# Earlier operands for the double blocks of a decoder's feed-forward stages, a one-step mean square, and a Silu placed ahead of the mixer's last linear

## The chip, the cores and the metric

The kernel runs on one core of a Trainium2 chip. Its engines work side by side, each through its own queue in order: TensorE (PE, with its weight loads listed as PEld), VectorE (DVE), ScalarE (ACT), GpSimd (POOL) and SyncE (SP, which issues the weight transfers). They meet through semaphores. The metric is the device time of one execution in microseconds; the kernel before takes 1538.5 us (median of 3 runs, 1538.31 to 1540.32).

## The reference

The kernel computes a decoder trunk of two layers on 256 tokens of width 1024, all in f32. With `D_FF = 2816`, each layer is

```python
x = x + 0.5 * swiglu(rmsnorm(x, norm_ffn1[i]), w_ffn1_up[i], w_ffn1_down[i])
h = rmsnorm(x, norm_mix[i])
x = x + token_mixers(h, ...)      # attention, gated recurrence, latent attention; gated, summed, @ w_out
x = x + 0.5 * swiglu(rmsnorm(x, norm_ffn2[i]), w_ffn2_up[i], w_ffn2_down[i])
gate = sigmoid(rmsnorm(x, norm_ple[i]) @ w_ple_gate[i])
x = x + gate * (p[i] @ w_ple_proj[i])
```

with a last `rmsnorm` behind both layers, and

```python
def rmsnorm(x, g): return x * rsqrt(mean(x * x) + EPS) * g
def swiglu(x, w_up, w_down):
    g, u = split(x @ w_up, 2)
    return (silu(g) * u) @ w_down
```

## The kernel before

**Split products.** PE multiplies numbers that are split in a high part (rounded) and a low part (the rest), three matmuls a product: `mm3` (L222 high by high, L223 high by low of the weights, L224 low by high). Each weight tile `raw` arrives by a transfer that SP issues; ACT casts it into `h` (L216) and DVE subtracts to get `l` (L217). The tiles of `h` and of `l` are pools of five, so a cast waits until PE has finished with the tile five before. Activations are split in the same way in `hl` (L229 cast on ACT, L230 subtraction on DVE).

**Feed-forward.** `ffn` goes through blocks of 256 hidden columns. A plain block multiplies the 256 tokens (two halves t = 0, 1) by its part of the up weights into `pu`; `hid` forms silu(g) * u (`sg` on ACT at L450, `hd` on DVE at L451); `hid_t` and `hl` transpose and split it into `fh`, `fl`; and `downs` adds the block before into `acc` with the down weights, two units `d` a block. In every stage but the first of layer 0 the blocks 2, 5 and 8 are double blocks (`wide_up`). These use fewer products: the inputs are seen as 2 by 2 parts a11, a12, a22 and four sums s1 to s4 of them, and the weights as parts `e` (the tiles of the pool we) and `o` (pool wo), each with a half lo and a half hi. Seven products, a11, s1, s2, s4, s3, a12, a22 in this order, each of 2 j by 2 q by 3 = 12 matmuls of 128x512, run against weight sums which `add` builds in place (L376, two DVE operations each, j = 0 and 1; 8 in a double block). In each product, for each j, ACT casts (L368), DVE subtracts (L369), PE multiplies; PE's lines L222 to L224 are the same as for a plain block. The names tell the product: `pu<-h,sh` are the products with sums.

**The activation sums.** `sums_x` (L321 to L337) forms the four sums once a stage from `rawx`, the scaled inputs before their split: L329 to L332 on DVE, each 128x512, then four casts `sh` (ACT) and four low parts `sl` (DVE, L230). It is called behind block 1, just ahead of the first double block. The second and third double block use the same sums.

**Norms.** `norm_sum` squares half a row on ACT (L417) with a sum; `norm_finish` adds the two half sums (L422 on DVE), `rsqrt` turns that into a mean plus EPS (L238 on DVE) and takes the power -1/2 on POOL (L239). There are 18 such roots of a whole row.

**Order.** The code is written in one order, but a scheduler with priorities places each instruction on its engine's queue, and it puts instructions that depend on little well ahead of where they stand in the code. So the order on an engine isn't the order of the code. ACT needs its function table switched between Silu, Exp, Ln and Sigmoid; each switch is an ACT_TABLE_LOAD in ACT's queue ahead of the activation that needs it.

Of the kernel before, what the change touches and what calls it, by code (L numbers as in the profile page):

```python
# [10 lines left out]
F32 = mybir.dt.float32  # L11
# [3 lines left out]
AF = mybir.ActivationFunctionType  # L15
OP = mybir.AluOpType
AX = mybir.AxisListType

DM, SEQ, DEPTH, DFF, PLE = 1024, 256, 2, 2816, 256
EPS = 1e-6  # L20
# [124 lines left out]
class Build:  # L145
# [206 lines left out]
    def wide_up(self, name, b):  # L352
        nc = self.nc
        e, o = self.wide_fetch(name, b)
# [6 lines left out]
        s1, s2, s3, s4 = self.sx_  # L361
# [12 lines left out]
        def add(d, dh, r, rh):  # L374
            for j in range(2):
                nc.vector.tensor_tensor(d[j][:, :, dh], d[j][:, :, dh], r[j][:, :, rh], op=OP.add)  # L376

        def keep(ps):
            c = self.tmt("pc")
            nc.scalar.copy(c, ps)  # L380
            return c
# [6 lines left out]
        p5 = keep(pb)  # L388
        add(e, lo, o, hi)
        prod(pa, s2, e, lo, False, False)  # L390
        u2 = keep(pa)
        prod(pb, s4, o, hi, False, True)
        nc.vector.tensor_tensor(u2, u2, pb, op=OP.add)
        add(e, hi, o, hi)
        prod(pa, s3, e, hi, False, False)
# [4 lines left out]
        mul(u2, u2, -1.0, p1, op0=OP.mult, op1=OP.mult)  # L400
        add(e, lo, o, lo)
        prod(pa, a22, e, lo, False, True)
# [10 lines left out]
    def norm_sum(self, t, half):  # L413
        nc = self.nc
        xs = self.x[:, t, half * 512:(half + 1) * 512]
        jk = self.tm.tile([128, 512], F32, name="jk", tag="tm")
        nc.scalar.activation(jk, xs, AF.Square, accum_out=self.ss[t][:, half:half + 1])  # L417

    def norm_finish(self, t):
        nc = self.nc  # L420
        s1 = self.small.tile([128, 1], F32, name="s1", tag="s1")
        nc.vector.tensor_tensor(s1, self.ss[t][:, 0:1], self.ss[t][:, 1:2], op=OP.add)  # L422
        self.rsqrt(self.rstd[t], s1, DM, 1)

# [3 lines left out]
    def ffn(self, name, gcol_next, mid=None, hook=None):  # L428
# [47 lines left out]
        for wide, b in plan(name, self.layer):  # L476
# [33 lines left out]
            hds = [hid(pu, t) for t in range(2)]  # L510
            if scaled and b == 0:
                sums = self.sums_x
            if b < FB - 1:
# [5 lines left out]
                self.hl(hh, ll, pt)  # L519
                if scaled and b == 1:  # L520
                    sums()
            else:
# [572 lines left out]
    def mixer(self, i, gcol_next):  # L1095
# [34 lines left out]

        self.scope.close()
        self.norm_begin_early(gcol_next)
        self.square_linear("w_out", consume)
# [167 lines left out]
```

## Time and profile before

| | value |
|---|---|
| median of the runs | 1538.5 us |
| profiled execution | 1538.71 us |
| its span, first to last instruction | 1536.9 us |
| mean granted clock of TensorE | 0.997 |
| PE / DVE / ACT busy | 1494.9 / 1113.8 / 925.9 us |
| HBM read over the span | 171 GB/s |
| chain that ended last | PE 82%, DVE 8%, ACT 7%, issue 2%, DMA 1% |

An engine's busy time is the sum of its instructions; for PE it holds the filling of the array too (0.39 us for a 128x512 matmul, while the next one starts some 0.23 us later), so a stall of PE is read from the distance of two starts. In the timelines, a bracket at the end of a row tells how long the engine was idle before it and which instruction released it. The granted clock is the share of full speed that TensorE had: 1.00 is 2.4 GHz, 0.50 is 1.2 GHz.

### The profile page before, as it was taken

The page shows a single profiled execution, that of the slowest core. Times are in us where ns is not written, and L with a number is a line of the kernel's source. Part 1 is how long each engine was busy: PE and PEld are TensorE (multiplying, and loading weights), DVE is VectorE, ACT ScalarE, POOL GpSimd, SP SyncE. Part 2 cuts the span into 40 slices and gives each one's busy share as a digit, 9 for nine tenths or more (in the row PEclk, how much of TensorE's full clock was granted, in tenths as well). Part 3 has the DMA queues.
Part 4 walks back from the last instruction along what each step waited for, and adds up shares of the span by engine and source line. Part 5 has one row for each costly group of instructions (what it writes and reads, how often), then busy time and mean ns, then how long its engine had stood idle before and what let it go on. Part 6 is the DMA issues. An engine that isn't in the chain of part 4 may idle for free.

```text
span 1536.9 us, 21608 instructions
## 1 busy us (share of the span) xinstructions
PE 1494.9 (97%) x8156; PEld 1235.3 (80%) x8156; DVE 1113.8 (72%) x1675; ACT 925.9 (60%) x1367; POOL 35.3 (2%) x48
## 2 busy tenths in 40 slices
PE   7999999999999998999999999999999999989997
PEld 6888888888888877888777888888888888778886
DVE  6555577677756679887788997676776566799876
ACT  6444486568565456656756665865775644656655
POOL 0000010000000000000000000100000000000000
PEclk9999999999999999999999999999999999999999
DMA  8666545344537553467535435553454385444462
GB/s 292 188 195 189 185 142 187 125 150 142 176 100 279 187 178 112 154 228 247 194 114 193 151 150 175 180 173 114 145 174 137 120 305 185 130 174 159 160 199 96
DMA packets 76473, 264.54 MB, mean 172 GB/s; under 512 B 8608, under 2 KB 9536, under 8 KB 76368
## 3 DMA queue, kind: packets, MB, share of 16 engines
q1 hardware_dynamic: 76144, 263.00, 51.1%
q8 instruction: 64, 1.05, 0.3%
q0 software_dynamic: 80, 0.11, 0.1%
q14 instruction: 41, 0.34, 0.1%
q10 hardware_dynamic: 144, 0.05, 0.0%
HBM read 262.08 MB, written 1.05 MB: 171 GB/s over the span
## 4 chain that ended last, share of the span: by engine, by line
PE 82%; DVE 8%; ACT 7%; issue 2%; DMA 1%; POOL 0%; SPq 0%; POOLq 0%; DVEq 0%; ACTq 0%
PE pu L223 18%; PE pu L222 18%; PE pu L224 18%; PE acc L223 5%; PE acc L224 5%; PE acc L222 5%; DVE l L369 2%; PE sq L224 2%; PE sq L223 2%; PE sq L222 2%; ACT h L216 2%; DVE l L217 1%; DVE wide L376 1%; PE pt L459 1%; ACT P L687 1%
## 5 line engine op out<-in xcount | busy, mean ns | idle before, releaser
L217 DVE TENSOR_TENSOR l<-raw,h 128x1024 fp32r<-128x1024 f32 (+3 forms) x440 | 512.6, 1179 | 230.9 <-ACT h L216 224.0
L216 ACT CAST h<-raw 128x1024 fp32r<-128x1024 f32 (+4 forms) x439 | 438.6, 1011 | 241.7 <-PE pu L224 132.5
L222 PE MATMUL pu<-h,xth 128*128 128x512 f32 (+3 forms) x1160 | 450.5, 389 | 12.7 <-DVE h L216 5.9
L223 PE MATMUL pu<-l,xth 128*128 128x512 f32 (+3 forms) x1160 | 442.2, 381 | 6.5 <-DVE l L369 4.4
L224 PE MATMUL pu<-h,xtl 128*128 128x512 f32 (+3 forms) x1160 | 439.4, 380 | 1.0 <-DVE xtl L230 1.0
L222 PEld LDWEIGHTS pu<-h,xth 128*128 128x128 f32 x1160 | 218.9, 189 | 53.2 <-ACT xth L232 5.9
L223 PEld LDWEIGHTS pu<-l,xth 128*128 128x128 f32 x1160 | 219.0, 189 | 43.8 <-DVE l L369 5.3
L224 PEld LDWEIGHTS pu<-h,xtl 128*128 128x128 f32 x1160 | 218.6, 188 | 39.1 <-DVE xtl L230 2.2
L368 ACT CAST h<-wide 128x1024 fp32r<-128x1024 f32 x126 | 126.6, 1051 | 65.8 <-PE acc L224 40.8
L369 DVE TENSOR_TENSOR l<-wide,h 128x1024 fp32r<-128x1024 f32 x126 | 147.9, 1220 | 9.3 <-ACT h L368 9.0
L223 PE MATMUL acc<-l,fh 128*128 128x512 f32 x352 | 138.1, 392 | 0.0
L224 PE MATMUL acc<-h,fl 128*128 128x512 f32 x352 | 137.7, 391 | 0.0
L222 PE MATMUL acc<-h,fh 128*128 128x512 f32 x352 | 134.1, 392 | 0.0
L376 DVE TENSOR_TENSOR wide<-wide 128x1024 f32<-128x1024 f32 x72 | 85.6, 1220 | 0.5
L223 PEld LDWEIGHTS acc<-l,fh 128*128 128x128 f32 x352 | 66.1, 188 | 15.1 <-DVE l L217 1.5
L224 PEld LDWEIGHTS acc<-h,fl 128*128 128x128 f32 x352 | 66.1, 188 | 13.3
L222 PEld LDWEIGHTS acc<-h,fh 128*128 128x128 f32 x352 | 66.1, 188 | 13.3
L223 PE MATMUL pu<-l,sh 128*128 128x512 f32 x144 | 58.2, 404 | 6.6 <-DVE l L369 5.6
L222 PE MATMUL pu<-h,sh 128*128 128x512 f32 x144 | 56.2, 397 | 1.6 <-ACT h L368 1.6
L224 PE MATMUL pu<-h,sl 128*128 128x512 f32 x144 | 56.8, 395 | 0.0
L223 PE MATMUL pu<-l,fh 128*128 128x512 f32 x128 | 50.8, 397 | 0.0
L222 PE MATMUL pu<-h,fh 128*128 128x512 f32 x128 | 50.4, 394 | 0.2 <-ACT pp L578 0.2
(269 smaller groups left out, 1821.8 us busy)
## 6 DMA issues: line engine op xcount, KB each, us to landing
raw<-in_weights_dram SPq DMA_DIRECT2D x374, 512.0 KB, 4.5
wide<-in_weights_dram SPq DMA_DIRECT2D x72, 512.0 KB, 5.5
raw<-in_weights_dram SPq DMA_DIRECT2D x48, 384.0 KB, 3.2
raw<-in_weights_dram SPq DMA_DIRECT2D x8, 320.0 KB, 3.1
raw<-in_weights_dram SPq DMA_DIRECT2D x8, 256.0 KB, 2.7
xin<-in_xt_dram SPq DMA_DIRECT2D x4, 256.0 KB, 7.7
x<-in_x_dram SPq DMA_DIRECT2D x2, 512.0 KB, 9.7
out_dram<-o SPq DMA_DIRECT2D x4, 256.0 KB, 2.2
```

The lines of the kernel that those rows point to most:

```text
L216: (copy or nc.scalar.copy)(h[:, :m], raw[:, :m])
L217: nc.vector.tensor_tensor(l[:, :m], raw[:, :m], h[:, :m].bitcast(F32), op=OP.subtract)
L222: mm(out, ah, bh, start=start, stop=False, skip_group_check=skip)
L223: mm(out, ah, bl, start=False, stop=False, skip_group_check=skip)
L224: mm(out, al, bh, start=False, stop=stop, skip_group_check=skip)
L368: nc.scalar.copy(h, src)
L369: nc.vector.tensor_tensor(l, src, h.bitcast(F32), op=OP.subtract)
L376: nc.vector.tensor_tensor(d[j][:, :, dh], d[j][:, :, dh], r[j][:, :, rh], op=OP.add)
L459: nc.tensor.transpose(pt[:, f, t * 128:(t + 1) * 128], hd[:, f * 128:(f + 1) * 128], self.ident)
L687: nc.scalar.activation(P[n, o], P[n, o], AF.Exp, bias=q[:, 3:4], scale=A_SCALE, accum_out=q[:, 4 + n:5 + n])
```

## The change

Three edits. First, `sums_x` is called behind block 0 instead of block 1, and in `wide_up` the third and the fourth weight sum are each written one product or more earlier, as soon as the tile that they overwrite has been read. Second, the scale 1/1024 of the mean goes into the squaring on ACT, and one DVE operation forms the mean and adds EPS, in place of two. Third, ahead of the norm and of the linear `w_out` at the end of the mixer stands a Silu of a one-column constant, whose result nothing uses.

```diff
@@ -387,18 +387,18 @@
         prod(pb, s1, e, lo, True, False)
         p5 = keep(pb)
         add(e, lo, o, hi)
+        add(e, hi, o, hi)
         prod(pa, s2, e, lo, False, False)
         u2 = keep(pa)
+        add(e, lo, o, lo)
         prod(pb, s4, o, hi, False, True)
         nc.vector.tensor_tensor(u2, u2, pb, op=OP.add)
-        add(e, hi, o, hi)
         prod(pa, s3, e, hi, False, False)
         u3 = keep(pa)
         prod(pc, a12, o, lo, True, True)
         nc.vector.tensor_tensor(p1, p1, pc, op=OP.add)
         nc.scalar.activation(p1, p1, AF.Silu)
         mul(u2, u2, -1.0, p1, op0=OP.mult, op1=OP.mult)
-        add(e, lo, o, lo)
         prod(pa, a22, e, lo, False, True)
         nc.vector.tensor_tensor(p5, p5, u3, op=OP.add)
         nc.scalar.activation(u3, pa, AF.Silu)
@@ -414,13 +414,13 @@
         nc = self.nc
         xs = self.x[:, t, half * 512:(half + 1) * 512]
         jk = self.tm.tile([128, 512], F32, name="jk", tag="tm")
-        nc.scalar.activation(jk, xs, AF.Square, accum_out=self.ss[t][:, half:half + 1])
+        nc.scalar.activation(jk, xs, AF.Square, scale=DM ** -0.5, accum_out=self.ss[t][:, half:half + 1])
 
     def norm_finish(self, t):
         nc = self.nc
-        s1 = self.small.tile([128, 1], F32, name="s1", tag="s1")
-        nc.vector.tensor_tensor(s1, self.ss[t][:, 0:1], self.ss[t][:, 1:2], op=OP.add)
-        self.rsqrt(self.rstd[t], s1, DM, 1)
+        ms = self.small.tile([128, 1], F32, name="ms", tag="ms")
+        nc.vector.scalar_tensor_tensor(ms, self.ss[t][:, 0:1], EPS, self.ss[t][:, 1:2], op0=OP.add, op1=OP.add)
+        nc.gpsimd.tensor_tensor(self.rstd[t], ms, self.mhalf[:, :1], op=OP.pow)
 
     def xmm(self, out, t, k, rh, rl, start, stop):
         self.mm3(out, self.xth[t][:, k, :], self.xtl[t][:, k, :], rh, rl, start, stop)
@@ -508,8 +508,6 @@
                     self.pending()
                 up(q, t)
             hds = [hid(pu, t) for t in range(2)]
-            if scaled and b == 0:
-                sums = self.sums_x
             if b < FB - 1:
                 if prev is not None:
                     downs()
@@ -517,8 +515,8 @@
                 for t in range(2):
                     hid_t(pt, hds[t], t)
                 self.hl(hh, ll, pt)
-                if scaled and b == 1:
-                    sums()
+                if scaled and b == 0:
+                    self.sums_x()
             else:
                 for pb, hT in prev[:-1]:
                     d0 = down_units(pb)
@@ -1129,6 +1127,8 @@
             self.norm_after(t, half)
 
         self.scope.close()
+        warm = self.small.tile([128, 1], F32, name="warm", tag="s1")
+        nc.scalar.activation(warm, self.mhalf[:, :1], AF.Silu)
         self.norm_begin_early(gcol_next)
         self.square_linear("w_out", consume)
```

How this moves instructions is read from the order on the engines. The first place is DVE in the second feed-forward stage of layer 0, from the `hd` of block 0's second half (`xs` are the sums, `sl` their low parts, `fl` the low part of the hidden values, `wide` the tiles e and o). Before:

```order
L451 TENSOR_TENSOR hd_5334<-pu_5237,sg_5333 128x256
L217 TENSOR_TENSOR l_5431<-raw_5428,h_5430 128x1024
L230 TENSOR_TENSOR fl_5263<-pt_5337,fh_5262 128x512
L217 TENSOR_TENSOR l_5437<-raw_5434,h_5436 128x1024
L369 TENSOR_TENSOR l_5515<-wide_5499,h_5514 128x1024
L376 TENSOR_TENSOR wide_5499<-wide_5499 128x2x512
L376 TENSOR_TENSOR wide_5499<-wide_5499,wide_5505 128x2x512
L451 TENSOR_TENSOR hd_5421<-pu_5344,sg_5420 128x256
L369 TENSOR_TENSOR l_5525<-wide_5502,h_5524 128x1024
L451 TENSOR_TENSOR hd_5425<-pu_5345,sg_5424 128x256
L329 TENSOR_TENSOR xs_5475<-xr1_5288 128x512
L376 TENSOR_TENSOR wide_5502<-wide_5502 128x2x512
```

After:

```order
L451 TENSOR_TENSOR hd_5324<-pu_5227,sg_5323 128x256
L329 TENSOR_TENSOR xs_5334<-xr1_5278 128x512
L217 TENSOR_TENSOR l_5445<-raw_5442,h_5444 128x1024
L230 TENSOR_TENSOR fl_5253<-pt_5327,fh_5252 128x512
L330 SCALAR_TENSOR_TENSOR xs_5335<-xs_5334,xr0_5174 128x512
L331 TENSOR_TENSOR xs_5336<-xr0_5174,xr1_5278 128x512
L332 SCALAR_TENSOR_TENSOR xs_5337<-xr0_5174,xs_5335 128x512
L230 TENSOR_TENSOR sl0_5343<-xs_5334,sh0_5342 128x512
L230 TENSOR_TENSOR sl1_5347<-xs_5335,sh1_5346 128x512
L230 TENSOR_TENSOR sl2_5351<-xs_5336,sh2_5350 128x512
L230 TENSOR_TENSOR sl3_5355<-xs_5337,sh3_5354 128x512
L217 TENSOR_TENSOR l_5451<-raw_5448,h_5450 128x1024
```

The sums and their low parts stood behind the two `hd` of block 1 and between the weight sums; now they stand directly behind the `hd` of block 0, ahead of the second down unit's `l` and of the double block's first.

The second place is DVE further on, in the same double block. The tiles of e are wide_5499 and wide_5502 before, wide_5489 and wide_5492 after; those of o are wide_5505 and wide_5508, then wide_5495 and wide_5498. Before:

```order
L376 TENSOR_TENSOR wide_5499<-wide_5499,wide_5505 128x2x512
L376 TENSOR_TENSOR wide_5502<-wide_5502,wide_5508 128x2x512 x2
L369 TENSOR_TENSOR l_5563<-wide_5499,h_5562 128x1024
L369 TENSOR_TENSOR l_5573<-wide_5502,h_5572 128x1024
L369 TENSOR_TENSOR l_5585<-wide_5505,h_5584 128x1024
L369 TENSOR_TENSOR l_5595<-wide_5508,h_5594 128x1024
L369 TENSOR_TENSOR l_5608<-wide_5499,h_5607 128x1024
L369 TENSOR_TENSOR l_5618<-wide_5502,h_5617 128x1024
L393 TENSOR_TENSOR pc_5582<-pc_5582,pu_5511 128x512
L369 TENSOR_TENSOR l_5630<-wide_5505,h_5629 128x1024
L369 TENSOR_TENSOR l_5640<-wide_5508,h_5639 128x1024
L376 TENSOR_TENSOR wide_5499<-wide_5499,wide_5505 128x2x512
```

After:

```order
L369 TENSOR_TENSOR l_5529<-wide_5489,h_5528 128x1024
L376 TENSOR_TENSOR wide_5492<-wide_5492,wide_5498 128x2x512
L230 TENSOR_TENSOR fl_5385<-pt_5482,fh_5384 128x512
L369 TENSOR_TENSOR l_5539<-wide_5492,h_5538 128x1024
L376 TENSOR_TENSOR wide_5489<-wide_5489,wide_5495 128x2x512
L376 TENSOR_TENSOR wide_5492<-wide_5492,wide_5498 128x2x512
L369 TENSOR_TENSOR l_5555<-wide_5489,h_5554 128x1024
L369 TENSOR_TENSOR l_5565<-wide_5492,h_5564 128x1024
L376 TENSOR_TENSOR wide_5489<-wide_5489,wide_5495 128x2x512
L376 TENSOR_TENSOR wide_5492<-wide_5492,wide_5498 128x2x512
L369 TENSOR_TENSOR l_5579<-wide_5495,h_5578 128x1024
L369 TENSOR_TENSOR l_5589<-wide_5498,h_5588 128x1024
```

In both orders six weight sums stand ahead of the `l` of s2 (l_5563 and l_5573 before, l_5555 and l_5565 after). The last two, which stood behind the `l` of a12 (l_5630, l_5640), now stand ahead of the `l` of s4 (l_5579, l_5589).

The third place is ACT in the attention part of the mixer of layer 0 (`ckh` and `kpeT` belong to the latent attention's keys, `PT` and `P` to the window attention's softmax). Before:

```order
L232 ACTIVATE ckh<-pt,gains 128x128
L705 COPY PT<-pt 128x384
L232 ACTIVATE ckh<-pt,gains 128x128
L954 COPY kpeT<-pt 64x128 x2
L232 ACTIVATE ckh<-pt,gains 128x128
L747 ACTIVATE bf<-pu,rstd 128x512
L705 COPY PT<-pt 128x384
L216 CAST h<-raw 128x768 x3
L229 CAST fh<-po 128x256
L687 ACTIVATE P,sta<-P,sta 128x384 x2
```

After:

```order
L1131 ACT_TABLE_LOAD
L1131 ACTIVATE warm<-mhalf 128x1
L232 ACTIVATE ckh<-pt,gains 128x128
L703 COPY PT<-pt 128x384
L232 ACTIVATE ckh<-pt,gains 128x128
L952 COPY kpeT<-pt 64x128 x2
L745 ACTIVATE bf<-pu,rstd 128x512
L232 ACTIVATE ckh<-pt,gains 128x128
L703 COPY PT<-pt 128x384
L216 CAST h<-raw 128x768 x3
L229 CAST fh<-po 128x256
L685 ACT_TABLE_LOAD
```

The one-column Silu `warm` does not stand ahead of `w_out`: it depends on a constant alone and stands in the mixer's middle, with a table load of its own, and the softmax behind it has a load that it did not have. In layer 1 it is the same, and the load at L450 stands in the order as before.

## Rows read from the trace of the kernel before

**Rows 1.** Page, busy time, share of the span and instructions of each engine
```profile
PE 1494.9 (97%) x8156; PEld 1235.3 (80%) x8156; DVE 1113.8 (72%) x1675; ACT 925.9 (60%) x1367; POOL 35.3 (2%) x48
```

**Rows 2.** Table of waits of PE: us in total, times, longest us
```profile
PE pu L223 <- DVE l L369: 10.0, 7, 1.8
```

**Rows 3.** Timeline of PE: start, us, instruction, [idle before <-releaser]
```profile
559.67 0.50 PE L222 MATMUL pu<-h,xth 128*128 128x512 f32 x1 [1.44 <-ACT xth L229]
...
577.58 0.39 PE L223 MATMUL acc<-l,fh 128*128 128x512 f32 x1
...
585.32 0.39 PE L222 MATMUL pu<-h,sh 128*128 128x512 f32 x1
585.81 0.50 PE L223 MATMUL pu<-l,sh 128*128 128x512 f32 x1
...
589.16 0.50 PE L222 MATMUL pu<-h,sh 128*128 128x512 f32 x1 [0.56 <-ACT h L368]
...
591.48 0.50 PE L223 MATMUL pu<-l,sh 128*128 128x512 f32 x1 [1.82 <-DVE l L369]
...
602.40 0.49 PE L222 MATMUL pu<-h,xth 128*128 128x512 f32 x1
...
604.36 0.50 PE L223 MATMUL pu<-l,xth 128*128 128x512 f32 x1 [1.46 <-DVE l L369]
```

**Rows 4.** Stretches: us; PE, PEld, DVE, ACT, POOL busy; PEclk; DMA; GB/s
```profile
582.50:607.00 24.50, 20.56 (x87) 15.59 (x85) 24.36 (x26) 16.80 (x22) 0.00 (x0) 1.00 0.19 62
811.00:816.00 5.00, 4.74 (x14) 3.74 (x15) 5.00 (x6) 3.52 (x5) 0.00 (x0) 0.66 0.00 0
```

**Rows 5.** Timeline of DVE, a first double block, layer 0
```profile
566.83 0.41 DVE L451 TENSOR_TENSOR hd<-pu,sg 128x256 f32<-128x256 f32 x1
...
570.29 1.23 DVE L217 TENSOR_TENSOR l<-raw,h 128x1024 fp32r<-128x1024 f32 x1 [1.20 <-ACT h L216]
572.52 1.23 DVE L369 TENSOR_TENSOR l<-wide,h 128x1024 fp32r<-128x1024 f32 x1 [1.01 <-ACT h L368]
...
577.98 0.68 DVE L329 TENSOR_TENSOR xs<-xr 128x512 f32<-128x512 f32 x1
...
581.53 2.49 DVE L230 TENSOR_TENSOR sl<-xs,sh 128x512 fp32r<-128x512 f32 x4
...
590.21 6.90 DVE L369 TENSOR_TENSOR l<-wide,h 128x1024 fp32r<-128x1024 f32 x6
```

**Rows 6.** Groups by line: busy us, mean ns, idle before <-releasers; the roots
```profile
L239 POOL TENSOR_TENSOR rstd<-ms,mhalf 128x1 f32<-128x1 f32 x18 | 9.9, 551 | 1073.4 <-ACT xth L232 566.9 <-DVE ms L238 486.7 <-ACT h L216 19.8
```

**Rows 7.** Timeline of DVE, the end of the program
```profile
1531.41 0.16 DVE L422 TENSOR_TENSOR s<-ss 128x1 f32<-128x1 f32 x1
1531.60 0.15 DVE L238 TENSOR_SCALAR ms<-s 128x1 f32<-128x1 f32 x1
```

**Rows 8.** Timeline of ACT, feed-forward stages
```profile
557.43 1.28 ACT L450 ACT_TABLE_LOAD   x1 [0.40 <-PE pu L224]
558.73 0.38 ACT L450 ACTIVATE sg<-pu 128x256 f32<-128x256 f32 x1
...
767.09 0.72 ACT L295 ACTIVATE xs<-x,rstd 128x512 f32<-128x512 f32 x1 [0.68 <-POOL rstd L239]
```

**Rows 9.** Timeline of ACT in the mixers of both layers
```profile
328.17 0.37 ACT L232 ACTIVATE ckh<-pt,gains 128x128 fp32r<-128x128 f32 x1 [0.67 <-DVE ckl L233]
...
329.89 0.48 ACT L705 COPY PT<-pt 128x384 f32<-128x384 f32 x1 [1.36 <-PE pt L700]
...
340.44 0.62 ACT L687 ACTIVATE P<-P,sta 128x384 f32<-128x384 f32 x1 [2.02 <-DVE sta L685]
...
1090.81 0.48 ACT L705 COPY PT<-pt 128x384 f32<-128x384 f32 x1 [1.52 <-PE pt L700]
```

**Rows 10.** Timeline of ACT, casts of the first double block
```profile
571.44 1.05 ACT L368 CAST h<-wide 128x1024 fp32r<-128x1024 f32 x1 [1.18 <-PE pu L224]
574.16 1.06 ACT L368 CAST h<-wide 128x1024 fp32r<-128x1024 f32 x1 [1.67 <-PE pu L224]
```


## The prediction

> **What bounds the kernel now.** I read the page's busy line first [rows 1]: TensorE (PE) is busy 1494.9 of 1536.9 us, VectorE (DVE) 1113.8. So an edit is worth only what it takes from PE's gaps; work taken off DVE or ScalarE (ACT) is worth nothing by itself. Next the table of waits for PE [rows 2]: its largest entry is PE at L223 waiting for `l` of L369, 10.0 us in 7 waits. That is one place of the program, met three times: the first double block of each of the three feed-forward stages that have double blocks. Then PE's own rows there [rows 3]. A 128x512 matmul starts every 0.23 us (from 591.48 to 602.40 there are 47 steps, 10.92 / 47 = 0.232), so each longer distance is a stall: 585.32 to 585.81 (0.49, stall 0.26), 585.81 to 589.16 (3.35 for 11 steps, which are 2.55: stall 0.8), 589.16 to 591.48 (2.09) and 602.40 to 604.36 (1.73), together 4.9 us. Two of these rows carry a wait for L369, 1.82 + 1.46 = 3.28; three such places make 9.8 of the 10.0 us of [rows 2], so the other two stages have the same stalls, and 3 x 4.9 = 14.7 us hang on the three places.
>
> Who is late there? The table of stretches [rows 4] says that DVE is busy 24.36 of the 24.50 us from 582.5 to 607, ACT only 16.80. DVE is simply behind. Its rows just before [rows 5] show where the time for it lies: between 566.83 and 577.98 it idles 1.20 us (before 570.29) and 1.01 us (before 572.52), for casts of ACT; then, where PE is about to need weight sums, it does four activation sums and their four low parts.
>
> **The double blocks, worked out.** The change puts these eight small operations behind the `hd` of 566.83, into the two idle stretches, and puts the last two weight sums (L376) ahead of the `l` of product s4; the six others already stand ahead of that of s2. DVE does the same operations as before; what it gains is the idle it no longer has, 1.20 + 1.01 = 2.2 us. The second and third double blocks of a stage get no sums, and their instructions on DVE stand practically as before; I count them at 0.
>
> What PE gets from it depends on the order, so I walk DVE's new order from 566.83 without idle up to the `l` of the third product's first half (row `l_5579` in the order after). That is 17 large operations (2 of L217, 7 of L369, 8 of L376), 10 small ones (4 sums, 4 `sl`, 2 `fl`), and 3 `hd`. From [rows 5]: a large one 6.90 / 6 = 1.15, a small one 2.49 / 4 = 0.62, an `hd` 0.41. So 17 x 1.155 + 10 x 0.62 + 3 x 0.42 = 19.6 + 6.2 + 1.3 = 27.1, and DVE reaches the end of that `l` at 593.9.
>
> On PE: product s1 starts at 585.32 as now, without its 0.26, and takes 12 x 0.23 = 2.75, so s2 could start at 588.1. The `l` of its second half comes 13 large, 10 small and 3 `hd` after 566.83, 22.5 us, at 589.3: about 1.0 of stall is left in s2. The next product's second matmul would then start near 592.0 and waits for the `l` at 593.9: a stall of 1.9. Behind it 36 matmuls lead to the second matmul of the last product, 36 x 0.232 = 8.4, at 602.3, with the later `l` just in time, against 604.36 now. So the block gains about 2.1 and keeps 1.0 + 1.9 of its 4.9. In words: the moved sums take the wait of 1.73 away from the last product and open one of 1.9 in the one after s2, since the last two weight sums now stand ahead of its `l`; what is left as a gain is DVE's recovered idle. Three times: **-6.3**. The bounds: 0 if DVE finds another wait where the idle was, 4.9 a block (-14.7) if every stall goes. I take the walk since it is made of measured durations and ends at the idle's own size.
>
> What hides the moved operations is the distance to what they now stand ahead of: the `l` of 570.29 moves to about 574.0 to 575.2, and PE, by [rows 3], meets it first at 577.58: 2.4 us of cover. If that cover were gone, each microsecond there would come straight back.
>
> **One step in the mean square.** 18 roots [rows 6] lose one small DVE operation each; from 1531.41 to 1531.60 [rows 7] the step takes 0.19. At the end nothing runs beside it: 0.19 in full. In the first feed-forward stage of layer 1 ACT idles 0.68 for the root at 767.09 [rows 8], and the other half of the tokens has the like: 2 x 0.19. In the other places casts or the table load of [rows 8] end later than the root; I give them 0.1 together. Sum **-0.7**, bounds 0 and 18 x 0.19 = 3.4.
>
> **The early Silu table.** The text of the change puts a one-column Silu ahead of the last linear of the mixer, so that the load at 557.43 (1.28 us, [rows 8]), for which PE waits 1.44 at 559.67 [rows 3], would be done before. The order says otherwise: the scheduler puts this activation, which depends on nothing but a constant, into the attention part of the mixer, near 328 in layer 0 and 1090 in layer 1. Exp, Ln and Sigmoid come behind it, and the load at L450 still stands before `sg`. So nothing is gained there, and each layer gets two more loads: the one for this Silu and one back to Exp at the softmax (L685 after). Both wait for nothing. The first falls where ACT idles 0.67 and 1.36 [rows 9]: 2.03 against 1.28 + 0.2, the 0.2 for the one-column activation being an estimate from DVE's one-column step of 0.19. The second falls into the 2.02 before 340.44. In layer 1 the idle before 1090.81 is 1.52. I take 0.25 a layer for the copy that comes later, **+0.5**; the bounds are 0 and all four on the path, 4 x (1.28 + 0.2) = 5.9.
>
> One rule speaks against that and gets a sum of its own. The row shows a load of 1.28 at 557.43 and the activation that needs it at 558.73, 0.02 behind its end [rows 8]. The Trainium skill, page "ScalarE: Activation LUTs", section "What ACT_TABLE_LOAD costs", states some 1283 ns for the load and another 1380 ns for a drain, 2.66 us for every switch. The load agrees with the row, the drain does not show in it. By the page four more switches would be up to 10.6 us where the rows allow 5.9.
>
> **The sum.** -6.3 - 0.7 + 0.5 = -6.5, from the profiled execution of 1538.71 (span 1536.9 and 1.8 around it): 1532.2; the median 1538.5 lies 0.2 lower, so **1532**. One thing I leave out of the sum: at 811 to 816 the granted clock was 0.66 on average [rows 4], that is at 1.2 instead of 2.4 GHz for about two thirds of these 5 us, right behind PE's stall; that lost some 1.7 us. The same stall at 591 and 1352 left the clock at full. If the new, shorter stalls leave it alone, 1530.5; if it falls in one more block, 1533.7.
>
> **Rivals.**
> 1. *All of it works*: 14.7 of stalls and three loads of 1.28 (3.8) go, and 0.7, and the 1.7 of the clock: 1518 (1538.7 - 14.7 - 3.8 - 0.7 - 1.7 = 1517.8). For it: every stall in [rows 3] waits for DVE or ACT. Against it: DVE has 24.36 of 24.50 us of work in the stretch, and only 2.2 of idle ahead; the order keeps the load.
> 2. *The added loads land on PE's path* in the mixer. For it: at 340.44 ACT and DVE work in turns on the softmax [rows 9], so a delay of ACT is handed on. Against it: the idle is there, and both loads come without a wait. Price 5.9 in place of 0.5: 1532 + 5.4 = 1537.4, no change.
> 3. *Each added switch stops ACT for as long again as its load*, 2 x 1.28, and the idle is too short for it: 4 x 2.56 = 10.2 in place of 0.5, 1542. For it no row speaks; against it is the 0.02 between load and use. The page of the Trainium skill named above is where this rule stands.
> 4. *Slower: the fourth sum sticks in ACT's queue.* ACT works in order, and in the new order a cast of the double block stands between the third `sh` and the fourth. Before, such casts wait for PE to give a buffer back: 1.18 until 571.44, the next 1.67 until 574.16 [rows 10]. The walk has `sl3` due near 573.2, right behind the cast of 571.44. If the cast ahead of the fourth `sh` is released one product later, everything behind `sl3` on DVE is 2.7 late, and the block loses 2.7 - 2.1 = 0.6: 1540; two releases later, 3.3 a block: 1538.7 - 0.2 + 10 = 1548. It decides as soon as the last `sh` comes over 2.1 us later than 573.2. Against it: the order of the casts among themselves is unchanged.
>
> **Chances.** Forecast 0.75, with its own range 1529.5 to 1535; rival 1 0.04; rival 2 0.13; rival 3 0.02; rival 4 0.05; 0.01 for none of these. A measurement of this kernel tells about 0.2% (3.1 us) from no change; so faster means under 1535.4. That is the forecast and rival 1: 0.79; no change is rival 2 and half of the rest: 0.15; slower is rivals 3 and 4 in part: 0.06. The range takes the forecast and, upward, rival 2 in most of its size: 1529 to 1537.
>
> **What the new profile would show.** Right: the `hd` at 566.83 followed by `xs` at once, no idle of over 0.5 us in DVE between 567 and 594; in s2 a stall near 1.0, in s4 one near 1.9, in the last product none, and the first double block's last product some 2 us earlier in each of the three stages; two more table loads per layer, at L1131 and L685, in ACT's idle, and the load at L450 still there with PE's wait at 559.67; the last step 0.19 shorter. Wrong: DVE waiting for `sh` of ACT near 573; PE waiting in the last product still; PE's waits in the mixer (330 to 360, 1090 to 1120) grown by over 1 us; or a clock under full in more than one of the three blocks.

## The result and the profile after

| | before | changed |
|---|---|---|
| median, runs beside each other | 1538.4 us (4 runs, 1537.73 to 1540.32) | 1527.55 us (4 runs, 1526.94 to 1527.86) |
| profiled execution, span | 1538.71, 1536.9 us | 1527.65, 1525.8 us |
| mean granted clock | 0.997 | 0.998 |

The ratio is 0.992, interval 0.9908 to 0.9932. Forecast was 1532.0 with a range of 1529 to 1537: faster, as said, but 11 us and not 6.5, and outside the range.

The busy line of the page after (engines in the columns of [rows 1]):

```profile
PE 1491.4 (98%) x8156; PEld 1234.8 (81%) x8156; DVE 1109.5 (73%) x1657; ACT 933.3 (61%) x1373; POOL 37.9 (2%) x48
```

Busy times hardly moved, so the 11 us are idle time of PE. The table of PE's waits says which (waiting and releasing line, us in total, times, longest):

```profile
PE pu L222 <- ACT xth L229: 4.5, 4, 1.4
PE pu L223 <- DVE l L369: 2.6, 8, 0.4
PE pu L222 <- ACT pc L380: 2.2, 3, 0.7
```

The 10.0 us of [rows 2] for `l` of L369 are 2.6 now, and a new wait of 2.2 us for ACT's copy `pc` stands beside it. The wait for `xth` behind the table load (4.6 before, of which [rows 3] shows one of 1.44) has stayed.

PE in the first double block of the second feed-forward stage of layer 0, which answers to [rows 3] (start, duration, instruction, idle before and releaser):

```profile
585.49 0.39 PE L222 MATMUL pu<-h,sh 128*128 128x512 f32 x1
...
588.21 0.39 PE L222 MATMUL pu<-h,sh 128*128 128x512 f32 x1
589.01 0.50 PE L223 MATMUL pu<-l,sh 128*128 128x512 f32 x1 [0.41 <-DVE l L369]
...
592.74 0.51 PE L222 MATMUL pu<-h,sh 128*128 128x512 f32 x1 [0.72 <-ACT pc L380]
...
593.59 0.50 PE L223 MATMUL pu<-l,sh 128*128 128x512 f32 x1 [0.35 <-DVE l L369]
...
601.68 0.39 PE L223 MATMUL pu<-l,xth 128*128 128x512 f32 x1
...
612.00 0.39 PE L222 MATMUL pu<-h,xth 128*128 128x512 f32 x1
```

The stall of 589.01 is 0.80 - 0.23 = 0.57, those of 592.74 and 593.59 are 0.88 and 0.62 (0.85 - 0.23), and the last product waits for nothing: its second matmul starts at 601.68 instead of 604.36. In this way, distance of two starts less 0.23, the stalls of the three first double blocks are 4.8 us each before and 2.1 us each after. The wait for `pc` costs nothing by itself: the matmul behind it waits for `l` until 593.59 in any case.

The length of a block says the same. From the first matmul of product s1 it is 110 matmuls to the one at 612.00 above, and in the trace before to this one:

```profile
614.78 0.40 PE L222 MATMUL pu<-h,xth 128*128 128x512 f32 x1
```

That is 614.78 - 585.32 = 29.46 us before and 612.00 - 585.49 = 26.51 us after. In the other two stages the same distance is 31.03 and 29.39 before (the first of them with the clock at half for a part) and 26.56 and 26.51 after. So each block is 2.9 to 3.0 us shorter, a little more than its stalls, since the steps just behind a stall are longer too (0.34 instead of 0.23).

DVE in the same place, which answers to [rows 5]:

```profile
567.02 0.42 DVE L451 TENSOR_TENSOR hd<-pu,sg 128x256 f32<-128x256 f32 x1
567.36 0.68 DVE L329 TENSOR_TENSOR xs<-xr 128x512 f32<-128x512 f32 x1
...
571.50 0.68 DVE L230 TENSOR_TENSOR sl<-xs,sh 128x512 fp32r<-128x512 f32 x1
573.91 1.22 DVE L217 TENSOR_TENSOR l<-raw,h 128x1024 fp32r<-128x1024 f32 x1
...
587.73 1.22 DVE L369 TENSOR_TENSOR l<-wide,h 128x1024 fp32r<-128x1024 f32 x1
...
592.32 1.22 DVE L369 TENSOR_TENSOR l<-wide,h 128x1024 fp32r<-128x1024 f32 x1
```

The sums stand right behind `hd`, all four `sl` follow without a gap, and from 567.02 to 596.86 no bracket appears: the two idle stretches of [rows 5] are filled. The `l` of product s4 starts at 592.32 and is done at about 593.5.

The stretches of [rows 4] (us, busy time of PE, PEld, DVE, ACT, POOL, then granted clock, DMA share, GB/s):

```profile
582.50:607.00 24.50, 23.02 (x101) 18.10 (x99) 24.29 (x26) 18.13 (x22) 0.00 (x0) 1.00 0.29 101
805.00:812.00 7.00, 5.94 (x24) 4.32 (x24) 7.00 (x7) 6.42 (x8) 0.00 (x0) 1.00 0.00 0
```

PE is busy 23.02 of 24.50 us where it was 20.56. The second row is the stretch behind the stalls of the second block, which come some 6 us earlier now (804.79 to 809.38): its clock is 1.00, where the stretch behind the stall, 811 to 816, had 0.66.

ACT in the mixer and at the first silu, which answers to [rows 9] and [rows 8]:

```profile
328.31 1.28 ACT L1131 ACT_TABLE_LOAD   x1
329.61 0.20 ACT L1131 ACTIVATE warm<-mhalf 128x1 f32<-128x1 f32 x1
...
339.19 1.28 ACT L685 ACT_TABLE_LOAD   x1
341.19 0.62 ACT L685 ACTIVATE P<-P,sta 128x384 f32<-128x384 f32 x1 [0.72 <-DVE sta L683]
...
557.60 1.28 ACT L450 ACT_TABLE_LOAD   x1 [0.67 <-PE pu L224]
558.89 0.38 ACT L450 ACTIVATE sg<-pu 128x256 f32<-128x256 f32 x1
```

Two more loads, as the order had shown, and the load of 557.60 is still there. Each is followed by its activation within 0.02 us where nothing else is waited for.

At the end of the program, before (first two rows, which stand behind those of [rows 7]) and then after:

```profile
1532.24 0.55 POOL L239 TENSOR_TENSOR rstd<-ms,mhalf 128x1 f32<-128x1 f32 x1 [5.23 <-DVE ms L238]
1532.83 0.49 DVE L1252 TENSOR_SCALAR o<-o,rstd 128x512 f32<-128x512 f32 x1 [1.07 <-POOL rstd L239]
```

```profile
1520.53 0.16 DVE L422 SCALAR_TENSOR_TENSOR ms<-ss 128x1 f32<-128x1 f32 x1
1520.77 0.55 POOL L423 TENSOR_TENSOR rstd<-ms,mhalf 128x1 f32<-128x1 f32 x1 [4.88 <-DVE ms L422]
1521.35 0.49 DVE L1252 TENSOR_SCALAR o<-o,rstd 128x512 f32<-128x512 f32 x1 [0.66 <-POOL rstd L423]
```

From the first small operation to the scaled output it took 1532.83 - 1531.41 = 1.42 us and takes 1521.35 - 1520.53 = 0.82: 0.60 less. Beside the operation itself, POOL's start behind `ms` came at 0.64 before and 0.24 after. But the end of the span does not move by as much: from the start of the last matmul (1527.99 before, 1517.12 after) it is 8.95 us before and 8.70 after, so 0.25 less, near the 0.19 of the prediction. The trace shows where the rest stays. Of the 18 roots before, 17 started 0.23 to 0.32 behind the start of `ms`, and only the last one 0.64; after, all start at 0.23 to 0.30, and a pause of 0.41 us stands among POOL's closing semaphore instructions, ahead of the very last one, where it was 0.06 before. What this pause is, no run shows.

**Where the 11.1 us between the two profiled executions went**, by the distance between the same matmuls in both traces: the three first double blocks -8.8 (-3.0, -2.9, -2.9); the clock near 811 -1.6; mean square -1.0 (0.25 at the end, 0.44 around the gate stage, 0.15 at the start of each second feed-forward stage); the two mixers -0.5 and +0.5; at the start of the program +0.8 and near 745 -0.5. The last two were different again in each later kernel, with or without the change: -0.1 to +1.2 and -0.5 to +0.3. The sum is -11.1.

### The profile page after: what moved, and what is told of

Read it like the earlier page. It is cut to its first block, busy times and chain, and to the rows that moved or that the text cites. A ratio compares the mean times of both kernels' runs of the same rounds, so it can differ in the third digit from the quotient of the medians.

```text
span 1525.8 us, 21598 instructions
## 1 busy us (share of the span) xinstructions
PE 1491.4 (98%) x8156; PEld 1234.8 (81%) x8156; DVE 1109.5 (73%) x1657; ACT 933.3 (61%) x1373; POOL 37.9 (2%) x48
## 4 chain that ended last, share of the span: by engine, by line
PE 80%; DVE 8%; ACT 7%; issue 3%; DMA 1%; POOL 0%; SPq 0%; POOLq 0%; DVEq 0%; ACTq 0%
PE pu L223 17%; PE pu L222 17%; PE pu L224 17%; PE acc L223 5%; PE acc L224 5%; PE acc L222 5%; DVE l L369 2%; DVE l L217 2%; ACT h L216 2%; PE sq L223 2%; PE sq L224 2%; PE sq L222 2%; DVE wide L376 1%; PE pt L459 1%; ACT P L685 1%
## 5 line engine op out<-in xcount | busy, mean ns | idle before, releaser
L369 DVE TENSOR_TENSOR l<-wide,h 128x1024 fp32r<-128x1024 f32 x126 | 148.0, 1218 | 6.5 <-ACT h L368 6.0
```

What stands on the lines that cost most here:

```text
L369: nc.vector.tensor_tensor(l, src, h.bitcast(F32), op=OP.subtract)
```

## The experiments

Eleven kernels were run. In the later comparisons the kernel before had medians from 1539.47 to 1541.22 us with single runs from 1538.04 to 1544.18; why they spread so far is a part of what the experiments show.

**The sums alone.**

```diff
-            if scaled and b == 0:
-                sums = self.sums_x
...
-                if scaled and b == 1:
-                    sums()
+                if scaled and b == 0:
+                    self.sums_x()
```

> Only the activation sums are moved behind block 0; weight sums, mean square and Silu stay as before. Theory (the gain of a first double block is DVE's recovered idle of 2.2 us and its queue's end, so the place of the last weight sums hardly matters): stalls in the three first double blocks fall from 4.8 to about 2 us each, as in the changed kernel, no stall above 1.0; total -8 to -10 us. Rival (the earlier weight sums carry a third or more of the gain): the last product keeps a wait of about 1.7 us and the total is -5 to -6. Clock: if the fall to half speed near 811 us hangs on the stall of 2.1 us ahead of it, it is gone here.

Measured: 1527.45 us against 1540.42 (27 runs), ratio 0.9916, interval 0.9903 to 0.993: 13 us, more than the 8 to 10 expected. It is as fast as the whole change. PE in the first double block:

```profile
589.35 0.50 PE L223 MATMUL pu<-l,sh 128*128 128x512 f32 x1 [0.65 <-DVE l L369]
...
592.80 0.50 PE L223 MATMUL pu<-l,sh 128*128 128x512 f32 x1 [0.39 <-DVE l L369]
...
601.35 0.50 PE L223 MATMUL pu<-l,xth 128*128 128x512 f32 x1
```

Stalls of 0.81, 0.56 and 0.26 us, 1.6 in all, and 1.4 in each of the two others; the clock is 1.00 in all three. Over the same 110 matmuls the blocks are shorter by 3.3, 3.5 and 3.5 us (with 1.6 for the clock taken off the second), 10.2 in all, where the whole change has 8.8. So the sums are nearly the whole gain. The rival of the earlier weight sums falls here, but not for the reason given: with the sums out of the way the scheduler by itself put one of the last two weight sums ahead of s4, the other ahead of the last product. Their place is tested below.

**The weight sums alone.**

```diff
         add(e, lo, o, hi)
+        add(e, hi, o, hi)
         prod(pa, s2, e, lo, False, False)
         u2 = keep(pa)
+        add(e, lo, o, lo)
         prod(pb, s4, o, hi, False, True)
...
-        add(e, hi, o, hi)
...
-        add(e, lo, o, lo)
```

> Only the weight sums are written earlier; activation sums as before. Theory: the wait moves from the last product (1.73) to the one after s2 (about 1.8), the stalls stay 4.6 to 4.9 us a block, total -0.6 to 0.3. Rival (earlier weight sums carry a part): -2 to -4 us. Clock: the stall of 2.1 us ahead of 811 is still there, so if the fall hangs on it, it comes again, here or in one of the two like places.

Measured: 1538.54 against 1540.42, ratio 0.9987, interval 0.9978 to 0.9996: about 1.9 us faster, between the two expectations. PE's waits in the first block, and three stretches of 7 us behind the stall in each of the three blocks (columns as above):

```profile
589.27 0.50 PE L222 MATMUL pu<-h,sh 128*128 128x512 f32 x1 [0.51 <-ACT h L368]
591.60 0.50 PE L223 MATMUL pu<-l,sh 128*128 128x512 f32 x1 [1.83 <-DVE l L369]
...
596.15 0.62 PE L222 MATMUL pu<-h,sh 128*128 128x512 f32 x1 [0.25 <-ACT pc L380]
597.09 0.50 PE L222 MATMUL pt<-h,xth 128*128 128x512 f32 x1 [0.32 <-ACT h L368]
```

```profile
590.00:597.00 7.00, 4.92 (x13) 3.18 (x13) 7.00 (x7) 5.93 (x7) 0.00 (x0) 0.76 0.00 0
809.00:816.00 7.00, 4.65 (x17) 3.25 (x16) 7.00 (x7) 5.84 (x7) 0.00 (x0) 0.92 0.00 0
1350.00:1357.00 7.00, 4.66 (x14) 3.20 (x13) 7.00 (x7) 5.46 (x7) 0.00 (x0) 0.80 0.00 0
```

The wait of the last product is gone, two of 0.65 and 0.72 (by starts) have come further on, and without the clock the stalls are 4.4 us instead of 4.8. (In the second stage, where the clock fell in both traces, the 110 matmuls take 30.1 us instead of 31.0.) The 2.1 at 591.60 is untouched, and behind it the clock fell in all three blocks. The profiled execution is this kernel's slowest, 1541.48, with a mean clock of 0.993; its fastest was 1537.35.

**The mean square alone.**

```diff
-        nc.scalar.activation(jk, xs, AF.Square, accum_out=self.ss[t][:, half:half + 1])
+        nc.scalar.activation(jk, xs, AF.Square, scale=DM ** -0.5, accum_out=self.ss[t][:, half:half + 1])
...
-        s1 = self.small.tile([128, 1], F32, name="s1", tag="s1")
-        nc.vector.tensor_tensor(s1, self.ss[t][:, 0:1], self.ss[t][:, 1:2], op=OP.add)
-        self.rsqrt(self.rstd[t], s1, DM, 1)
+        ms = self.small.tile([128, 1], F32, name="ms", tag="ms")
+        nc.vector.scalar_tensor_tensor(ms, self.ss[t][:, 0:1], EPS, self.ss[t][:, 1:2], op0=OP.add, op1=OP.add)
+        nc.gpsimd.tensor_tensor(self.rstd[t], ms, self.mhalf[:, :1], op=OP.pow)
```

> Only the mean square in one operation. Theory: -0.2 at the end of the program, -0.4 to -0.9 between the gate stage and the first feed-forward stage of layer 1, total -0.5 to -1.2; the stalls of the double blocks as before. Rival: no place on the path but the last, -0.2. Clock: the fall near 811 is still there if it hangs on the stall; if it hangs on chance, it may be missing.

Measured: 1538.71 against 1540.42, ratio 0.9988, interval 0.9979 to 0.9997, so 0.5 to 3.2 us. In the trace it takes 0.19 before the second feed-forward stage of layer 0, 0.42 around the gate stage, 0.14 before that of layer 1 and 0.26 at the end of the span: 1.0 us. The clock did fall, but in another place than before (same stretches):

```profile
590.00:597.00 7.00, 5.17 (x23) 4.08 (x23) 7.00 (x7) 7.00 (x9) 0.00 (x0) 1.00 0.00 0
809.00:816.00 7.00, 5.17 (x23) 4.06 (x23) 7.00 (x7) 7.00 (x9) 0.00 (x0) 1.00 0.00 0
1350.00:1357.00 7.00, 5.97 (x19) 4.76 (x20) 6.65 (x6) 5.57 (x8) 0.00 (x0) 0.76 0.00 0
```

The stall ahead is the same 2.10 us in all three blocks. So the same stall is followed by a fall in one block and not in another, and which one changes from trace to trace.

**The Silu alone.**

```diff
         self.scope.close()
+        warm = self.small.tile([128, 1], F32, name="warm", tag="s1")
+        nc.scalar.activation(warm, self.mhalf[:, :1], AF.Silu)
```

> Only the one-column Silu in front of the mixer's last linear, which the scheduler puts into the middle of the mixer. Theory (prediction): two more table loads per layer, mostly in ACT's idle, +0.5 in all, 0 to 1; the wait of 1.4 us at the first silu of the second feed-forward stage is unchanged. Rival (what the changed kernel showed in layer 0, 0.5 less in the mixer, is due to the order that the new activation brings): -0.5 in layer 0, +0.5 in layer 1, sum 0. Clock: as for the kernel with the mean square alone.

Measured: 1541.11 against 1540.42, ratio 1.0, interval 0.999 to 1.0009. In the trace the mixers give -0.2 and -0.1; the added loads are hidden. Neither expectation had it quite: the theory's +0.5 does not show, and the -0.5 and +0.5 of the changed kernel's mixers are not the Silu's (the kernel with the sums alone, which has no such Silu, gives -0.3 and +0.3 there). In the second of the three blocks the clock fell (0.76 from 809 to 816), in the other two it did not.

**Sums and mean square together**, without the other two parts (the two diffs above).

> The early activation sums and the one-step mean square, without the earlier weight sums and without the Silu. Theory (the other two parts are worth nothing): as fast as the changed kernel or up to 1.5 us faster, since the mean square takes 0.6 at the end of the program, 0.4 around the gate stage and 0.1 twice: 1526.0 to 1527.5. Rival (the parts need each other): over 1528.5.

Measured: 1526.39 against 1540.19, ratio 0.9917, interval 0.9903 to 0.9931. The changed kernel in its own session had 1527.55. So the other two parts bring nothing when the scheduler happens to place the last weight sums well. By the lengths of the blocks the early weight sums even cost something here: the three blocks are 10.2 us shorter than before in this kernel and 8.8 in the changed one.

**A Silu that depends on late values.**

```diff
+    def warm(self, src):
+        w = self.small.tile([128, 1], F32, name="warm", tag="s1")
+        self.nc.scalar.activation(w, src, AF.Silu)
...
             self.norm_after(t, half)
+            if (t, half) == (0, 0):
+                self.warm(self.ss[0][:, 0:1])
...
+            if (t, half) == (1, 1) and gcol_next is not None:
+                self.warm(g[:, 0:1])
```

> As the kernel with the sums and the mean square, and a one-column Silu that depends on late values: on the first half sum of squares in the mixer's last linear, and on the last gate of the gate stage of layer 0. So its table load cannot be drawn ahead of other functions, and the load at the first silu goes. Theory (the Silu of the change failed only by its place): PE's wait of 1.4 us at the first silu falls by 0.5 to 1.28 in three places, total 1.5 to 3.5 us under the kernel without it. Rival (what PE waits for there is not the load but the root and the casts): within 0.5 us.

Measured: 1528.63 against 1540.19, ratio 0.993, interval 0.9917 to 0.9942; 2.2 us slower than without it in the same session, which neither expectation had. The load at L450 is gone, and PE's waits say what came instead:

```profile
559.63 0.44 PE L463 MATMUL pt<-ident,hd 128*128 128x128 f32 x2 [0.71 <-DVE xr L309]
560.28 0.50 PE L222 MATMUL pu<-h,xth 128*128 128x512 f32 x1 [0.21 <-ACT xth L229]
...
589.50 0.50 PE L223 MATMUL pu<-l,sh 128*128 128x512 f32 x1 [0.73 <-DVE l L373]
...
602.38 0.50 PE L223 MATMUL pu<-l,xth 128*128 128x512 f32 x1 [1.46 <-DVE l L373]
```

At the first silu PE's wait for `xth` fell from 1.44 to 0.21, but a wait of 0.71 for DVE's `xr` came ahead: `hd` now stands ahead of `xr` in DVE's order (558.55 and 558.89), where it stood behind it without the late Silu (`xr` at 558.57, `hd` at 559.88). And the last product's wait of 1.46 is back: this time the scheduler left both last weight sums ahead of it. The stalls are 2.6 in each block, where the kernel without it had 1.4 to 1.6. So the place of the last weight sums is worth about a microsecond a block after all, and the expectation of the first run, that it hardly matters, was wrong. This kernel also shows the sums without any help of the weight sums, which stand in the order of before: its blocks are 2.3 us shorter each, with the clock taken off, close to DVE's recovered idle of 2.2.

**Work put back on DVE** where the sums had stood, on the kernel with the sums alone; nothing uses its result.

```diff
+                if scaled and b == 1:
+                    w = self.tmt("xs")
+                    v = ll.rearrange("p f t -> p (f t)").bitcast(F32)
+                    nc.vector.tensor_tensor(w, v, v, op=OP.add)
+                    for j in range(3):
+                        nc.vector.tensor_tensor(w, w, v, op=OP.add)
```

> The early activation sums alone, with four idle additions of 128x512 on DVE (0.6 us each, result unused) that depend on block 1 and so stand in the first double block where the sums stood before. Theory (a first double block ends when DVE's queue ends, so each microsecond of DVE work there comes straight back): stalls rise from 1.5 to about 3.5 to 4 a block; total +6 to +8 us plus 1.5 for each block in which the clock falls again, 1534 to 1540; and the spread between runs grows. Rival (the gain came from the place of the sums, not from DVE's backlog): under 1531. For the clock: if the stall ahead of it is what makes it fall, granted clocks under 1 show again in some of the three places; if it is something else in the old order, they stay at 1.

Measured: 1536.06 against 1540.19, ratio 0.9977, interval 0.9969 to 0.9986: 8.6 us over the kernel with the sums alone (1527.45, in another session), for 12 small operations of 0.6, 7.2 us. PE, and the clock behind the stall of s2 in the three blocks:

```profile
590.62 0.50 PE L223 MATMUL pu<-l,sh 128*128 128x512 f32 x1 [1.89 <-DVE l L369]
...
603.77 0.50 PE L223 MATMUL pu<-l,xth 128*128 128x512 f32 x1 [1.23 <-DVE l L369]
```

```profile
590.00:597.00 7.00, 6.38 (x27) 5.02 (x28) 7.00 (x8) 6.19 (x7) 0.00 (x0) 1.00 0.00 0
808.00:816.00 8.00, 6.86 (x29) 5.43 (x30) 8.00 (x9) 6.71 (x8) 0.00 (x0) 1.00 0.00 0
1347.00:1355.00 8.00, 6.84 (x29) 5.41 (x30) 8.00 (x9) 6.74 (x8) 0.00 (x0) 1.00 0.00 1
```

Stalls of 4.5, 4.3 and 4.2 us, up by 2.9 a block, of which the additions are 2.4; in this order both last weight sums stand ahead of the last product again, whose wait of 1.50 is the other part. DVE's work there comes straight back. What was expected of the clock did not show in this trace: the stall of s2 is 2.16 again, and no fall follows. The profiled execution, 1534.54, is the fastest of 11 and shows a clock of 1.00 in all three blocks; the others go up to 1539.28, with mean clocks of 0.999 down to 0.996.

**The late Silu with the place of the weight sums fixed**: first as in the change, then half of them each way (`add` takes the halves as a last argument), then the latter without any early Silu.

```diff
         u2 = keep(pa)
+        add(e, lo, o, lo, (0,))
         prod(pb, s4, o, hi, False, True)
...
-        add(e, lo, o, lo)
+        add(e, lo, o, lo, (1,))
         prod(pa, a22, e, lo, False, True)
```

> The kernel with the late Silu (1528.6), now with the weight sums written early as in the change. In the late-Silu kernel both last weight sums stood ahead of the last product again and its wait of 1.73 was back; here they stand ahead of product s4. Theory (with the activation sums out of the way, the place of the last two weight sums decides between 2.7 and about 2.0 of stall a block): 0.6 x 3 = 2 us faster, 1526.2 to 1527.2. Rival (the late Silu itself costs the 2 us): no change, 1528 to 1529.

> As the kernel with late Silu, but the last two weight sums written apart: the first half ahead of product s4, the second ahead of the last product, as the scheduler had placed them in the kernel with the sums alone. Theory: stalls of about 1.4 a block, so 1.2 x 3 = 3.7 us under the kernel with late Silu: 1524.5 to 1525.5, the fastest so far. Rival: 1528 to 1529.

> As the one before, without any early Silu, so with the table load at the first silu. Theory: the place is the one that the scheduler had found by itself, so as the kernel with sums and mean square, 1526.0 to 1527.0, and the late Silu is worth 1 to 1.8 us by the difference to the one before. Rival: the late Silu is worth nothing, the two are equal.

Measured, against 1539.47: 1527.34 (ratio 0.9915, interval 0.9901 to 0.993), 1525.72 (0.9908, 0.9896 to 0.9921) and 1526.34 (0.991, 0.9898 to 0.9923). Stalls of a first double block: 2.3, 1.6 to 1.7, and 1.4 to 1.6. The order of the three is as the theory had it, the sizes are smaller: fixing the weight sums gives 1.3 and 2.9 us (against 1528.63, in another session) where 2 and 3.7 were expected, and the late Silu 0.6 instead of 1 to 1.8. The medians of the last two differ by about as much as their single runs do (1525.4 to 1526.83 and 1525.8 to 1526.81). The second is the fastest kernel of the study; its table of PE's waits shows the trade at the silu, 4.5 us for `xth` turned into 1.0 and 1.9:

```profile
PE pt L464 <- DVE xr L309: 1.9, 3, 0.7
PE pu L222 <- ACT xth L229: 1.0, 4, 0.4
```

**More work on DVE**, six idle additions instead of four (the loop runs five times).

> As the kernel with four idle additions on DVE in each first double block, now with six (1.2 us more). Theory of DVE's backlog: 1.2 x 3 = 3.6 us slower than with four, 1538 to 1541. Clock: with four, the profiled execution showed 1.00 in all three places though its times spread over 4.7 us; with a longer stall the fall should be seen in the trace, in at least one of the three places behind the stall of s2. Rival: the fall belongs to the old order and has nothing to do with the stall, all three at 1.00 and a spread under 1 us.

Measured: 1541.19 against 1541.22, ratio 1.0001, interval 0.9991 to 1.0011: 5.1 us over the one with four in another session, where the additions alone are 3.6; by the two ratios, each against the kernel before in its own session, the step is 0.0024 of 1540, 3.7 us. The stretches behind the stall of the three blocks:

```profile
590.00:597.00 7.00, 5.49 (x17) 4.40 (x18) 7.00 (x9) 5.55 (x7) 0.00 (x0) 0.76 0.00 0
810.00:818.00 8.00, 6.11 (x19) 4.59 (x19) 8.00 (x10) 6.62 (x8) 0.00 (x0) 0.79 0.00 0
1350.00:1358.00 8.00, 6.12 (x23) 4.31 (x22) 8.00 (x10) 6.75 (x8) 0.00 (x0) 0.89 0.00 0
```

The clock fell in all three, and a second time near 828 and 1371, behind the last product's stall of 1.5 us. The stall of s2 was not longer than with four additions, though (2.15 to 2.17 against 2.16), since the two new additions stand behind its `l` in DVE's order. So this run does not test a longer stall: it shows the same stall, put back on the early sums, followed by a fall in three blocks where the other trace had none. The profiled execution is its slowest, 1544.18, mean clock 0.993.

## Why the prediction was wrong

The direction was right, and so was most of the mechanism: the sums filled the two idle stretches of DVE, the load at L450 stayed, the added loads were hidden, the wait left the last product and came up at s4. What failed are four terms of the sum, all on the same side; the largest are the one for the double blocks and the clock.

1. *The double blocks* ("So the block gains about 2.1", three times -6.3). Each block became 2.9 shorter, -8.8 in all, and kept 2.1 of stalls instead of 2.9. Two steps of the walk were too long. From `hd` at 567.02 to the end of that `l` at about 593.5 DVE took 26.5, not 27.1: the walk divided merged rows by their count (1.155 and 0.62), which counts the end of the last operation in; from start to start the rows of both traces give 1.13 to 1.14 (four `l` from 592.32 to 596.86) and 0.60. And behind that `l` it is 35 matmuls to the second one of the last product, not 36, since in PE's new order the `h` matmul of 592.74 stands ahead of the one that waits: 601.68 - 593.59 = 8.1 instead of 8.4. That is 0.9 a block.
   The reason given for the walk, that it "ends at the idle's own size", was chance. Recovered idle is only a part of the gain: with the last weight sums in their old place a block gained 2.3 (the late Silu), with both ahead of s4 2.9 (the changed kernel) or 2.7 (the late Silu with early weight sums), and with one ahead of s4 and one ahead of the last product 3.3 to 3.5 (the sums alone). So the earlier weight sums, to which the text gave no gain of their own, add 0.4 to 0.6 a block to the idle's 2.3, and not the most that their place can give.
2. *The clock, left out of the sum.* The text had its price of 1.7 us and an 1530.5 for it, but took the likeliest as "unchanged". The measured price is 1.6 (110 matmuls with the fall take 31.0 to 31.1 us, without it 29.4 to 29.5, in three traces). The experiments show that the fall is no trait of one place. Where s2's second half waits 2.1 us, the clock to half behind it was seen in 1 of 3 blocks before, in 3 with the weight sums alone, 1 with the mean square alone, 1 with the Silu alone, 0 and 3 with DVE's work put back. Where that wait is under 1 us, it was seen in none of the blocks (the changed kernel, the sums alone, and the five others with early sums and no added work). Shown: the falls come with the long stall and go with it. Not settled: why some executions have none and others three.
   That goes with the spread. Kernels with the long stall spread over 4 to 6 us in nine or more runs, those without over 0.7 to 1.7 in four or five, and 2.8 in one case. Of the 27 runs of the kernel before in one session, the 12 with a mean clock of 0.994 or 0.995 have a median of 1542.0 us, the 12 with 0.997 or 0.998 one of 1539.3. So the falls make a large part of the spread of the kernel before, its median holds some of them, and a single profiled execution couldn't tell how many. One run of 1530.0 of the kernel with the sums alone, at a clock of 0.998, is not explained by this.
3. *The mean square* ("-0.7"): -1.0. The end of the program (0.25 for 0.19) and the gate stage (0.44 for 2 x 0.19) were close; the start of each second feed-forward stage, where the text gave nearly nothing, gained 0.15.
4. *The early Silu* ("+0.5"): nothing that the runs can tell. The idle of [rows 9] took it whole. The Trainium skill, page "ScalarE: Activation LUTs", section "What ACT_TABLE_LOAD costs", adds a drain of about 1380 ns to each load; it does not show here either: `warm` starts 0.02 us behind its load's end at 328.31 + 1.28.

Summed, with the +0.3 at the start of the program and near 745 that no part of the change explains: 1532.2 - 2.5 - 1.6 - 0.3 - 0.5 + 0.3 = 1527.6, against 1527.65 in the profiled execution. Each was within what the text allowed for, and none alone leaves the range (the double blocks alone would have given 1529.7), but the range was set as if they would not fall together; rival 1, with 0.04, was the only case below 1529.

Of the rivals, none came. The fourth `sh` stood at 572.63 in ACT's queue, right behind the cast at 571.67, as the walk had it.

What the change's parts are worth: the sums alone 10 us and the clock, the mean square 1.0, the Silu nothing. The weight sums are worth 0.4 a block alone, by its stalls. Beside the sums they fix a place: better than the one with both ahead of the last product, worse (by some 1.4 us over the three blocks) than the split that the scheduler sometimes finds by itself.

## What to carry to other kernels

Where a gain is the small difference of two long chains, take the durations from start to start of the same operations, walk the new order of both engines, and give the difference the error of the chains, not of the gain. A stall that is followed by a fall of the clock costs more than its length, and in only some executions; when a change removes the stall, count the falls in, and read the spread of the runs beside the one profile. That a sum comes out near a quantity that seems to explain it is no proof: vary one of the two. Where a scheduler sets the order, an operation whose only input is a constant does not stay where it is written, and an unrelated edit can move others: tie both to data, or check the order.

## What the runs showed of the hardware

TensorE's granted clock went to its lower level (1.2 of 2.4 GHz) behind PE's stall of 2.1 us in 9 of 18 blocks; the stretches above show means of 0.66 to 0.92 there. The same stall left it at 1.00 in other blocks, also of the same execution, and no block whose wait there was under 1 us (21 in seven traces) shows a fall. Table loads of 1.28 us and a one-column activation of 0.20 us cost nothing that the runs can tell (ratio 1.0, interval 0.999 to 1.0009) where ACT idled for 2.0 us. On DVE, a 128x1024 operation took 1.13 to 1.14 us and a 128x512 one 0.60 from start to start in a chain, where single rows read 1.22 and 0.68.
